# A hybrid decoder layer on one core: two projections in half-size products over all sixteen feature tiles, with seventeen early weight tiles

## The chip, the cores and the metric

The kernel runs on one core of a Trainium2 chip. The metric is the device time of one execution in microseconds (us); less is better. Engines: TensorE (PE) for matrix products, VectorE (DVE) and ScalarE (ACT) for elementwise work, GpSimd (POOL) and SyncE (SP) for little more than the issue of transfers. A "cast" below is ACT's copy of an fp32 tile to the rounded format that PE multiplies.

## The reference

One decoder layer for x of 512 tokens by 2048 features, in float32:

```python
h = rmsnorm(x, g)
p = h @ w_in                      # (512, 2048) @ (2048, D_IN), split by IN_SPLITS
# attention group: q, keys and values for three branches, branch gates, a gate path z_a of 1024 columns
# HGRN2 group: q, forget gate f, values i (1024 columns), a gate path z_h
o = concat(nsa(...) * silu(z_a), hgrn2(...) * silu(z_h))   # each head normalised first
y = rmsnorm(x + o @ w_out, g_final)
```

What matters here are two of the column groups of w_in, each of 1024 columns: HGRN2's values (from column C_IH on) and the attention's gates (from C_ZA on). Each is a product of h (512 x 2048) with a 2048 x 1024 piece of w_in.

## The kernel before

**Precision.** Every fp32 operand is split in two rounded parts, a high part (the cast, L304, on ACT) and a low part (the rest, L305, on DVE); the function is parts(), and a product takes three matmuls: high by high, high by low, low by high. The transposed, normalised input lies in SBUF as hh and hl, sixteen feature tiles of 128 x 512 each.

**The order of the program.** Small projections of the keys and values come first (second_proj and proj_tm, up to L586), then the two large projections of this case in seven products each, then blocks() (L611 to L625), make_kd, make_q and the compression of keys and values (L632 to L641), then attention, HGRN2 and the output. Each engine works off its own list of instructions in order; the lists are made when the program is built, from the order of the code and from when buffers come free.

**Seven products.** seven() (L406) splits a 512 x 1024 projection in a 2 x 2 block form: the tokens in two halves of 256, the columns in two halves of 512, and the feature tiles in pairs, of which one member is the first and the other the second half of the inner dimension. By Strassen's rule in Winograd's form seven half-size products do for eight; their left operands are sums of blocks of the input (sums_of, L365 to L377, made once, while the projection of V runs), their right operands sums of weight blocks. PAIRS says how many pairs of feature tiles go this way, 6 of 8 before; the last four feature tiles go through rest(), as plain products into the same banks.

A projection is a list of steps, each with a part that prepares and a part that multiplies. Two pairs make a step. first(jj) loads three weight blocks of 128 x 1024 (L419), makes two differences (L410) and three pairs of parts; it feeds three products. second(jj) and third(jj) load one block, add one (L411), and make two pairs of parts for two products each. A step of rest() loads one block (L163) and makes one pair of parts for 24 plain matmuls (L466 to L468). The half-size products stand at L456 to L458. in_turn() runs the steps and prepares AHEAD7 = 2 steps ahead of the step that multiplies, over both projections in one list. After a group of steps the sums of the products are taken out of PSUM: after_first, after_second, after_third, after_all, by DVE additions (L411 again, on 128 x 512 tiles called e), and then scaled (L535, v_done) or put through a tanh (L541 and L542, z_done). third_sums() keeps one corner of the input aside in DRAM and writes a sum over it; block_21_back() (L401) brings it back during the second projection.

**Buffers.** Weight tiles are 128 x 1024 in float32, 4 KB a partition. b4() takes them by turns from two pools, w with WBUF = 10 tiles and, in this first part of the kernel, more_w with NU = 10. The space of more_w and of the sums goes to other tiles after the two projections.

**Behind the projections.** blocks() brings the keys for compression back from DRAM with eight transfers that ACT issues (L611 to L614) and adds position vectors to them on DVE (L625, sixteen additions). make_kd(0, 0) and make_q(0) project keys and queries with weight tiles of eight feature tiles by 128 columns (proj_fm, L559 to L561, two tiles a projection, 24 matmuls a tile); split_dma (L686 to L691) then spreads the result over partitions by transfers that SP issues. compress() (L632 to L641) loads its own weights through SP too.

Of the kernel before, what the change touches and what calls it, by code (L numbers as in the profile page):

```python
# [30 lines left out]
WBUF = 10  # L31
# [2 lines left out]
PJ = 4  # L34
AHEAD = 2
FILL = (44, 42, 40, 24)
NU = 10
NE = 8
PAIRS = 6
AHEAD7 = 2  # L40
KWB = 4
EVA = "AD"
# [6 lines left out]
def hymba_layer(ctx: ExitStack, tc: tile.TileContext, x, norm_in, w_in, pe_k, w1_k, w2_k,  # L49
# [12 lines left out]
    cnt = [0, 0, 0]  # L62

    def nm(s):
        cnt[0] += 1
        return f"{s}_{cnt[0]}"


    space, first_part = {}, ExitStack()
# [11 lines left out]
    def dram(shape=(P, 512)):  # L81
        n = nm("d")
        return scr.tile(list(shape), FP32, name=n, tag=n, bufs=1)
# [6 lines left out]

    def b4(dt):
        cnt[2] += 1
        if "more_w" in space and cnt[2] % 2:
            return space["more_w"].tile([P, WCOLS], dt, name=nm("w"), tag="w", bufs=NU)
        return space["w"].tile([P, WCOLS], dt, name=nm("w"), tag="w", bufs=WBUF)

# [64 lines left out]
    def load_raw(src, k0, kt, c0, c):  # L161
        raw = b4(FP32)[:, 0:kt * c].rearrange("p (k c) -> p k c", k=kt)
        nc.sync.dma_start(out=raw, in_=src[k0 * P:(k0 + kt) * P, c0:c0 + c].rearrange("(k p) c -> p k c", p=P))  # L163
        return raw
# [4 lines left out]
    for k0, kt in FIRST:  # L169
        cs = slice(k0 * P, (k0 + kt) * P)  # L170
        first_w.append(load_raw(w_in2, k0, kt, C_KC, 256))
        if kt == 2:
            w = b4(FP32).rearrange("p (t c) -> p t c", t=4)
            for i in range(2):
                nc.sync.dma_start(out=w[:, 2 * i:2 * i + 2],
                                  in_=x2[i * 256:(i + 1) * 256, cs].rearrange("(t p) c -> p t c", p=P))
            xt.append([w[:, t] for t in range(NT)])
        else:
            w = [b4(FP32).rearrange("p (t c) -> p t c", t=2) for _ in range(2)]
            xt.append([w[t // 2][:, t % 2] for t in range(NT)])  # L180
            for t in range(NT):
                nc.sync.dma_start(out=xt[-1][t], in_=x2[t * P:(t + 1) * P, cs])
# [125 lines left out]
    def load_w(src, k0, kt, c0, c, to=None):  # L308
        return parts(load_raw(src, k0, kt, c0, c), to)
# [43 lines left out]

    a21 = [[dram((P, 2, 256)) for _ in range(PAIRS // 2)] for _ in range(2)]
    sums, s3 = {}, {}
# [28 lines left out]
    def all_sums():  # L384
        for j in range(PAIRS):
            sums_of(j)
            yield 1.0

    def third_sums():

        for q in range(PAIRS // 2):
            for part in range(2):
# [5 lines left out]
    def block_21_back():  # L398
        for q in range(PAIRS // 2):
            for part in range(2):  # L400
                nc.gpsimd.dma_start(out=corner(q, part).bitcast(FP32), in_=a21[part][q])  # L401
# [4 lines left out]
    def seven(c0, done, then=lambda: None):  # L406
# [36 lines left out]
        def give(*names):  # L443
            for name in names:
                free_banks.append(banks[name])

        def products(jj, ops, names):
            for (left, bank, fresh), (hi, lo) in zip(names, ops):
                if jj == 0 and fresh:
                    take(bank)  # L450
                for tt in range(2):
                    ts = slice(tt * P, (tt + 1) * P)
                    o = acc[bank][tt]
                    for j in range(2):
                        ah, al = [a[:, ts] for a in sums[2 * jj + j][left]]
                        nc.tensor.matmul(o, ah, hi[:, j], start=fresh and jj + j == 0, stop=False, skip_group_check=True)  # L456
                        nc.tensor.matmul(o, al, hi[:, j], start=False, stop=False, skip_group_check=True)  # L457
                        nc.tensor.matmul(o, ah, lo[:, j], start=False, stop=jj + 1 == PAIRS // 2 and j == 1,  # L458
                                         skip_group_check=True)

        def plain(k0, w, outs):
            hi, lo = w
            for t in range(NT):
                for k in range(2):
                    ah, al = [hT[part][k0 + k][:, t * P:(t + 1) * P] for part in range(2)]
                    nc.tensor.matmul(outs[t], ah, hi[:, k], start=False, stop=False, skip_group_check=True)  # L466
                    nc.tensor.matmul(outs[t], al, hi[:, k], start=False, stop=False, skip_group_check=True)
                    nc.tensor.matmul(outs[t], ah, lo[:, k], start=False, stop=k0 + k == NK - 1, skip_group_check=True)  # L468
# [20 lines left out]
        def after_third():  # L489
            for tt in range(2):  # L490
                add(room["u2"][tt], acc["5"][tt], room["u2"][tt])

        def after_all():
            for tt in range(2):
                y = room["u2"][tt]
                add(y, acc["3"][tt], y)
                done(1, tt, y, y)
            for tt in range(2):
                y = room["u3"][tt]
                add(y, acc["5"][tt], y)  # L500
                done(1, 2 + tt, y, y)
            give("5", "3")

        def group(prepare, names, after):
            steps = [(lambda jj=jj: prepare(jj), lambda ops, jj=jj: products(jj, ops, names)) for jj in range(PAIRS // 2)]
            return steps[:-1] + [(steps[-1][0], lambda ops: (steps[-1][1](ops), after()))]

        def rest(right, names, after):
            steps = []
            for k0 in range(2 * PAIRS, NK, 2):  # L510
                def mul(w, k0=k0):
                    plain(k0, w, [acc[n][tt] for n in names for tt in range(2)])
                    if k0 + 2 == NK:
                        after()
                steps.append((lambda k0=k0: load_w(w_in2, k0, 2, c0 + 512 * right, 512), mul))
            return steps

        return (group(first, (("A11", "1", True), ("S2", "6", True), ("S3", "7", True)), after_first) +
                group(second, (("A22", "4", True), ("A12", "1", False)), lambda: None) + rest(0, "14", after_second) +
                group(third, (("S1", "5", True), ("S4", "3", True)), after_third) + rest(1, "35", after_all))  # L520
# [632 lines left out]
    with tc.manual_schedule(engines={mybir.EngineType.PE, mybir.EngineType.Activation, mybir.EngineType.DVE}):  # L1153
# [5 lines left out]
         70), (all_sums(), 7))  # L1159
    third_sums()  # L1160
    in_turn(seven(C_IH, v_done) + seven(C_ZA, z_done(0), block_21_back))
    first_part.close()
    del space["more_w"]
# [139 lines left out]
```

## Time and profile before

| | us |
|---|---|
| median of three runs | 1102.68 |
| lowest and highest run | 1102.62, 1103.29 |
| the profiled execution | 1100.78 |
| its span | 1099.1 |
| PE busy in it | 1073.5 (98%) |
| DVE busy | 658.8 (60%) |
| ACT busy | 419.6 (38%) |
| POOL busy | 95.5 (9%) |

The span runs from the first to the last instruction of the profiled execution, the time of an execution has a little around it. The mean granted clock of PE in it was 0.994 of full speed. Shares of busy time are averages over stages that differ; what a stage waits for is read from the timeline of that stage. Matmuls overlap: one of 512 columns lasts 0.39 us in the timeline, and the next starts 0.23 us behind it.

### The profile page before, as it was taken

What the parts mean: (1) busy time and instruction counts of PE and PEld (TensorE: products, weight loads), DVE (VectorE), ACT (ScalarE), POOL (GpSimd) and SP (SyncE); (2) the same over time, 40 slices, a digit from 0 to 9 for tenths busy, and PEclk for the clock granted to TensorE, in tenths of its full rate; (3) what the DMA queues carried; (4) which work ended last, traced back from release to release, by engine and by line L of the source; (5) the groups of instructions that cost most, each with busy time, mean ns of one, the idle gap of its engine ahead of it and who ended that gap; (6) DMA issues with size and microseconds to landing.
All of it is one profiled execution on the core that took longest, in us unless ns stands there. A gap on an engine that the chain in (4) does not pass through costs nothing.

```text
span 1099.1 us, 15254 instructions
## 1 busy us (share of the span) xinstructions
PE 1073.5 (98%) x5610; PEld 883.3 (80%) x5610; DVE 658.8 (60%) x1549; ACT 419.6 (38%) x835; POOL 95.5 (9%) x170
## 2 busy tenths in 40 slices
PE   7999999999989999999999999999999999999996
PEld 6799888888868777777877887888888888888886
DVE  4767656764344676576765565666666788424332
ACT  6534443442123665555553222222222443324211
POOL 1000000101521020110200000000000000202010
PEclk9999999999999999999999999999999999999999
DMA  9435346444685222222212323221222723335223
GB/s 317 146 119 161 118 134 209 155 163 130 195 267 139 71 61 59 62 73 58 58 40 78 95 68 105 78 77 58 77 61 63 248 90 106 113 109 172 96 86 124
DMA packets 100010, 127.45 MB, mean 116 GB/s; under 512 B 6672, under 2 KB 62368, under 8 KB 99936
## 3 DMA queue, kind: packets, MB, share of 16 engines
q1 hardware_dynamic: 94368, 113.90, 33.8%
q0 software_dynamic: 2624, 8.39, 2.1%
q10 hardware_dynamic: 2944, 4.19, 1.1%
q8 instruction: 44, 0.72, 0.3%
q14 instruction: 30, 0.25, 0.1%
HBM read 106.01 MB, written 12.06 MB: 107 GB/s over the span
## 4 chain that ended last, share of the span: by engine, by line
PE 90%; DVE 5%; DMA 2%; issue 2%; ACT 1%; SPq 0%; ACTq 0%; POOL 0%; DVEq 0%; POOLq 0%
PE pj L559 8%; PE pj L560 8%; PE pj L561 8%; PE pj L584 7%; PE pj L586 7%; PE pj L585 7%; PE ot L826 4%; PE pj L807 3%; PE lp L975 2%; PE pj L458 2%; PE pj L457 2%; PE pj L456 2%; PE lp L793 2%; PE lp L641 2%; PE lp L794 1%
## 5 line engine op out<-in xcount | busy, mean ns | idle before, releaser
L305 DVE TENSOR_TENSOR w<-w,w 128x1024 fp32r<-128x1024 f32 (+3 forms) x169 | 204.4, 1215 | 188.9 <-ACT w L304 88.3
L304 ACT CAST w<-w 128x1024 fp32r<-128x1024 f32 (+3 forms) x169 | 173.0, 1036 | 276.3 <-DMA w<-in_w_in_dram 148.4
L559 PE MATMUL pj<-hh,w 128*128 128x512 f32 x448 | 183.5, 410 | 2.8 <-ACT w L304 2.2
L560 PE MATMUL pj<-hl,w 128*128 128x512 f32 x448 | 178.6, 399 | 0.0
L561 PE MATMUL pj<-hh,w 128*128 128x512 f32 x448 | 176.7, 394 | 0.5 <-DVE w L305 0.5
L584 PE MATMUL pj<-w,hh 128*128 128x512 f32 (+2 forms) x352 | 127.1, 361 | 0.0
L585 PE MATMUL pj<-w,hl 128*128 128x512 f32 (+2 forms) x352 | 125.8, 358 | 0.0
L586 PE MATMUL pj<-w,hh 128*128 128x512 f32 (+2 forms) x352 | 125.6, 357 | 0.0
L559 PEld LDWEIGHTS pj<-hh,w 128*128 128x128 f32 x448 | 84.3, 188 | 21.1 <-issue 2.9
L561 PEld LDWEIGHTS pj<-hh,w 128*128 128x128 f32 x448 | 84.2, 188 | 19.0 <-issue 1.2
L560 PEld LDWEIGHTS pj<-hl,w 128*128 128x128 f32 x448 | 84.4, 188 | 15.9 <-issue 1.3
L767 ACT ACTIVATE s<-s,mn 128x128 f32<-128x128 f32 (+3 forms) x128 | 71.6, 560 | 28.1 <-DVE mn L762 18.6
L762 DVE CUSTOM_DVE_ANT_0 s<-s,lp 128x128 f32<-128x128 f32 (+3 forms) x128 | 60.3, 482 | 35.9 <-PE lp L794 32.8
L586 PEld LDWEIGHTS pj<-w,hh 128*128 128x128 f32 x352 | 66.5, 189 | 8.5
L584 PEld LDWEIGHTS pj<-w,hh 128*128 128x128 f32 x352 | 66.5, 189 | 8.1
L585 PEld LDWEIGHTS pj<-w,hl 128*128 128x128 f32 x352 | 66.5, 189 | 8.0
L807 PE MATMUL pj<-ident,s 128*128 128x128 f32 x320 | 53.8, 274 | 0.4 <-ACT s L767 0.3
L816 ACT COPY pt<-pj 128x256 f32<-128x256 f32 (+2 forms) x56 | 25.6, 457 | 57.4 <-PE pj L807 57.2
L826 PE MATMUL ot<-pt,s 128*64 128x512 f32 (+3 forms) x256 | 47.3, 440 | 0.0
L807 PEld LDWEIGHTS pj<-ident,s 128*128 128x128 f32 x320 | 39.6, 140 | 9.5 <-ACT s L767 3.0
L826 PEld LDWEIGHTS ot<-pt,s 128*64 128x64 f32 x256 | 22.8, 136 | 21.2 <-issue 11.3
L584 PE MATMUL pj<-w,s 128*128 128x512 f32 x96 | 37.7, 392 | 0.0
(346 smaller groups left out, 1912.0 us busy)
## 6 DMA issues: line engine op xcount, KB each, us to landing
w<-in_w_in_dram SPq DMA_DIRECT2D x121, 512.0 KB, 3.5
w<-in_w_out_dram SPq DMA_DIRECT2D x32, 512.0 KB, 3.6
s<-s SPq DMA_DIRECT2D x48, 128.0 KB, 2.3
w<-in_x_dram SPq DMA_DIRECT2D x16, 256.0 KB, 6.4
d<-e POOLq DMA_DIRECT2D x12, 256.0 KB, 3.1
l<-in_x_dram SPq DMA_DIRECT2D x12, 256.0 KB, 5.1
out_dram<-l SPq DMA_DIRECT2D x12, 256.0 KB, 3.1
w<-in_w_in_dram SPq DMA_DIRECT2D x5, 456.0 KB, 3.2
```

The costliest lines, as they stand in the source:

```text
L304: nc.scalar.copy(hi, raw)
L305: nc.vector.tensor_tensor(lo, raw, hi.bitcast(FP32), ALU.subtract)
L559: nc.tensor.matmul(acc[j], wh, hh, start=kk == 0, stop=False)
L560: nc.tensor.matmul(acc[j], wh, hl, start=False, stop=False)
L561: nc.tensor.matmul(acc[j], wl, hh, start=False, stop=kk == NK - 1)
L584: nc.tensor.matmul(o, ah, hi[:, k, :], start=kk == 0, stop=False)
L585: nc.tensor.matmul(o, al, hi[:, k, :], start=False, stop=False)
L586: nc.tensor.matmul(o, ah, lo[:, k, :], start=False, stop=kk == NK - 1)
L762: nc.vector.tensor_tensor_reduce(out=y, in0=e["bias"][:, 384 - i * P:512], in1=lp, scale=1.0, scalar=3e38, op0=ALU.add, op1=ALU.min, accum ...
L767: nc.scalar.activation(y, y, AF.Exp, bias=mn, scale=-1.0, accum_out=e["ls"][:, 2 * i + b:2 * i + b + 1])
L807: nc.tensor.transpose(tps[:, j * P:(j + 1) * P], y[:, j * P:(j + 1) * P], ident)
L826: nc.tensor.matmul(e["ot"][b * 64:(b + 1) * 64, j * P:512], v_tok[j][:, b * 256 + g * DH:b * 256 + (g + 1) * DH], e["pt"][:, b, j * 512:38 ...
```

## The change

All sixteen feature tiles go through the half-size products: PAIRS is 8, each group has four steps in place of three, and rest() is empty. The sums of two more pairs of the input are made and kept, which takes 12 KB a partition; more_w has seven tiles in place of ten, and b4() deals the tiles out in the ratio of seven to ten. Without steps in rest(), after_second comes behind the second group itself, and after_third and after_all come together behind the third. All lines behind L517 move down by 4.

```diff
--- before.py
+++ after.py
@@ -34,9 +34,9 @@
 PJ = 4
 AHEAD = 2
 FILL = (44, 42, 40, 24)
-NU = 10
+NU = 7
 NE = 8
-PAIRS = 6
+PAIRS = 8
 AHEAD7 = 2
 KWB = 4
 EVA = "AD"
@@ -90,7 +90,7 @@
 
     def b4(dt):
         cnt[2] += 1
-        if "more_w" in space and cnt[2] % 2:
+        if "more_w" in space and cnt[2] * NU % (NU + WBUF) < NU:
             return space["more_w"].tile([P, WCOLS], dt, name=nm("w"), tag="w", bufs=NU)
         return space["w"].tile([P, WCOLS], dt, name=nm("w"), tag="w", bufs=WBUF)
 
@@ -515,6 +515,10 @@
                 steps.append((lambda k0=k0: load_w(w_in2, k0, 2, c0 + 512 * right, 512), mul))
             return steps
 
+        if not rest(0, "14", None):
+            return (group(first, (("A11", "1", True), ("S2", "6", True), ("S3", "7", True)), after_first) +
+                    group(second, (("A22", "4", True), ("A12", "1", False)), after_second) +
+                    group(third, (("S1", "5", True), ("S4", "3", True)), lambda: (after_third(), after_all())))
         return (group(first, (("A11", "1", True), ("S2", "6", True), ("S3", "7", True)), after_first) +
                 group(second, (("A22", "4", True), ("A12", "1", False)), lambda: None) + rest(0, "14", after_second) +
                 group(third, (("S1", "5", True), ("S4", "3", True)), after_third) + rest(1, "35", after_all))
```

A projection has 336 matmuls in place of 348. The lists of the engines change most at two places, and SP's behind them. In the rows below w is a weight tile, e an eviction tile of 128 x 512, pj, lp, tp and ot PSUM banks, s a tile of the second part, d scratch in DRAM; the number behind a name tells tiles of one kind apart. L535, L541, L542, L611 and L625 of before are L539, L545, L546, L615 and L629 of the change.

**DVE, from the end of the first projection to the start of the second.** Before:

```order
L305 TENSOR_TENSOR w_1725<-w_1719,w_1724 128x1024
L305 TENSOR_TENSOR w_1729<-w_1722,w_1728 128x1024
L411 TENSOR_TENSOR e_1422<-pj_1625,e_1422 128x512
L411 TENSOR_TENSOR e_1423<-pj_1626,e_1423 128x512
L305 TENSOR_TENSOR w_1733<-w_1717,w_1732 128x1024
L410 TENSOR_TENSOR w_1762<-w_1762,w_1760 128x1024
L410 TENSOR_TENSOR w_1767<-w_1762,w_1764 128x1024
L305 TENSOR_TENSOR w_1770<-w_1764,w_1769 128x1024
L305 TENSOR_TENSOR w_1774<-w_1767,w_1773 128x1024
L305 TENSOR_TENSOR w_1778<-w_1762,w_1777 128x1024
L411 TENSOR_TENSOR e_1422<-lp_1639,e_1422 128x512
L411 TENSOR_TENSOR e_1423<-lp_1640,e_1423 128x512
```

The sums over e_1422 to e_1425 are after_third and after_all of the first projection; w_1725 to w_1733 are low parts of the first step of the second projection, w_1762 to w_1778 its second step. Both steps stand ahead of the last sums. With the change:

```order
L411 TENSOR_TENSOR e_1514<-pj_1693,e_1514 128x512
L411 TENSOR_TENSOR e_1516<-pj_1693,e_1516 128x512
L411 TENSOR_TENSOR e_1515<-pj_1694,e_1515 128x512
L411 TENSOR_TENSOR e_1514<-lp_1707,e_1514 128x512
L410 TENSOR_TENSOR w_1758<-w_1758,w_1756 128x1024
L411 TENSOR_TENSOR e_1515<-lp_1708,e_1515 128x512
L410 TENSOR_TENSOR w_1763<-w_1758,w_1760 128x1024
L305 TENSOR_TENSOR w_1766<-w_1760,w_1765 128x1024
L411 TENSOR_TENSOR e_1517<-pj_1694,e_1517 128x512
L305 TENSOR_TENSOR w_1770<-w_1763,w_1769 128x1024
L305 TENSOR_TENSOR w_1774<-w_1758,w_1773 128x1024
```

Here e_1514 to e_1517 are the sums and w_1758 to w_1774 the first step of the second projection. The sum over lp_1708 waits for the last product of the first projection, and the subtraction that makes w_1763 and the low parts w_1766, w_1770 and w_1774 stand behind it.

**ACT, at the same place.** Before, the casts of the first two steps and then the scalings of the last sums:

```order
L304 CAST w_1724<-w_1719 128x1024
L304 CAST w_1728<-w_1722 128x1024
L304 CAST w_1732<-w_1717 128x1024
L304 CAST w_1769<-w_1764 128x1024
L304 CAST w_1773<-w_1767 128x1024
L304 CAST w_1777<-w_1762 128x1024
L535 ACTIVATE e_1422<-e_1422,rs 128x512
L535 ACTIVATE e_1423<-e_1423,rs 128x512
L536 DMA d_160<-e_1422 128x512
L536 DMA d_161<-e_1423 128x512
```

With the change:

```order
L304 CAST w_1728<-w_1721 128x1024
L304 CAST w_1724<-w_1368 128x1024
L539 ACTIVATE e_1516<-e_1516,rs 128x512
L540 DMA d_164<-e_1516 128x512
L539 ACTIVATE e_1514<-e_1514,rs 128x512
L540 DMA d_162<-e_1514 128x512
L304 CAST w_1765<-w_1760 128x1024
L539 ACTIVATE e_1515<-e_1515,rs 128x512
L304 CAST w_1769<-w_1763 128x1024
L304 CAST w_1773<-w_1758 128x1024
L540 DMA d_163<-e_1515 128x512
```

The scaling of e_1514, whose sum is the fourth row on DVE above, stands ahead of the cast w_1765, which the first product of the second projection takes.

**ACT, from the second projection to make_kd.** Before, four weight tiles of make_kd and make_q, then the last tanhs and the transfers of blocks():

```order
L304 CAST w_2445<-w_2443 128x1024
L304 CAST w_2475<-w_2473 128x1024
L304 CAST w_2524<-w_2522 128x1024
L304 CAST w_2554<-w_2552 128x1024
L541 ACTIVATE e_2332<-e_1976,rs 128x512
L541 ACTIVATE e_2337<-e_1977,rs 128x512
L541 ACTIVATE e_2342<-e_1978,rs 128x512
L611 DMA s_2364<-d_500 64x512
```

With the change:

```order
L545 ACTIVATE e_2385<-e_2076,rs 128x512
L616 DMA s_2417<-d_502 64x511
L545 ACTIVATE e_2390<-e_2077,rs 128x512
L545 ACTIVATE e_2395<-e_2078,rs 128x512
L545 ACTIVATE e_2400<-e_2079,rs 128x512
L617 DMA s_2418<-d_502 64x512
L618 DMA s_2418<-d_502 64x511
L615 DMA s_2423<-d_503 64x512
L616 DMA s_2423<-d_503 64x511
L617 DMA s_2424<-d_503 64x512
L618 DMA s_2424<-d_503 64x511
L304 CAST w_2528<-w_2526 128x1024
```

The tiles w_2445 and w_2475 of before are the two of make_kd(0, 0), w_2524 and w_2554 those of make_q(0). The other seven transfers and the fourth tanh follow behind. With the change w_2498 and w_2528 are the two of make_kd(0, 0); w_2498 and one transfer stand just ahead of these rows, and w_2528 stands behind all eight transfers.

**DVE, at the same place.** Before:

```order
L305 TENSOR_TENSOR w_2446<-w_2443,w_2445 128x1024
L305 TENSOR_TENSOR w_2476<-w_2473,w_2475 128x1024
L411 TENSOR_TENSOR e_1976<-pj_2193,e_1976 128x512
L411 TENSOR_TENSOR e_1977<-pj_2194,e_1977 128x512
L305 TENSOR_TENSOR w_2525<-w_2522,w_2524 128x1024
L305 TENSOR_TENSOR w_2555<-w_2552,w_2554 128x1024
L411 TENSOR_TENSOR e_1976<-pj_2207,e_1976 128x512
L411 TENSOR_TENSOR e_1977<-pj_2208,e_1977 128x512
L542 SCALAR_TENSOR_TENSOR e_1976<-e_2332,e_1976 128x512
```

With the change:

```order
L305 TENSOR_TENSOR w_2499<-w_2496,w_2498 128x1024
L411 TENSOR_TENSOR e_2077<-pj_2286,e_2077 128x512
L546 SCALAR_TENSOR_TENSOR e_2076<-e_2385,e_2076 128x512
L546 SCALAR_TENSOR_TENSOR e_2077<-e_2390,e_2077 128x512
L546 SCALAR_TENSOR_TENSOR e_2078<-e_2395,e_2078 128x512
L546 SCALAR_TENSOR_TENSOR e_2079<-e_2400,e_2079 128x512
L629 TENSOR_TENSOR s_2429<-s_2417,col 128x4x31
L629 TENSOR_TENSOR s_2429<-s_2418,col 128x4x31
...
L629 TENSOR_TENSOR s_2432<-s_2423,col 128x4x31
L305 TENSOR_TENSOR w_2529<-w_2526,w_2528 128x1024
L629 TENSOR_TENSOR s_2429<-s_2424,col 128x4x31
```

The low parts w_2446, w_2476, w_2525 and w_2555 stood ahead of the last sums. With the change only w_2499 does; w_2529, the low part of make_kd's second tile, stands behind twelve rows of L629.

**SP, from make_kd to the compression.** L163 loads weights, L632 compression's, L691 spreads kd (64 rows a transfer). Before:

```order
L163 DMA w_2552<-in_w_in_dram 128x8x128
L163 DMA w_2595<-in_w_in_dram 128x8x128
L632 DMA w_2613<-in_cmp_w_k_dram 128x4x256
L632 DMA w_2628<-in_cmp_w_k_dram 128x4x256
L632 DMA w_2650<-in_cmp_w_k_dram 128x4x256
L691 DMA s_2503<-s_2508 64x512 x2
L691 DMA s_2504<-s_2509 64x512 x2
L691 DMA s_2505<-s_2508 64x512 x2
```

With the change, where L636 and L695 are these lines:

```order
L163 DMA w_2605<-in_w_in_dram 128x8x128
L163 DMA w_2648<-in_w_in_dram 128x8x128
L695 DMA s_2556<-s_2561 64x512 x2
L695 DMA s_2557<-s_2562 64x512 x2
L695 DMA s_2558<-s_2561 64x512 x2
L695 DMA s_2559<-s_2562 64x512 x2
L636 DMA w_2666<-in_cmp_w_k_dram 128x4x256
L636 DMA w_2681<-in_cmp_w_k_dram 128x4x256
```

Three of the compression's weight tiles stood ahead of the transfers that spread kd; with the change all of them stand behind.

## Rows read from the trace of the kernel before

**Rows 1.** The page: busy time by engine, granted clock in 40 slices, chain that ended last.

```profile
PE 1073.5 (98%) x5610; PEld 883.3 (80%) x5610; DVE 658.8 (60%) x1549; ACT 419.6 (38%) x835; POOL 95.5 (9%) x170
...
PEclk9999999999999999999999999999999999999999
...
PE 90%; DVE 5%; DMA 2%; issue 2%; ACT 1%; SPq 0%; ACTq 0%; POOL 0%; DVEq 0%; POOLq 0%
```

**Rows 2.** Windows: us; busy PE, PEld, DVE, ACT, POOL (count); clock, DMA share, GB/s.

```profile
70.00:112.60 42.60, 42.60 (x326) 42.60 (x325) 24.55 (x34) 16.55 (x28) 0.00 (x0) 1.00 0.45 144
...
112.80:270.10 157.30, 157.30 (x695) 130.26 (x694) 100.22 (x99) 61.23 (x69) 7.01 (x11) 1.00 0.46 148
...
300.00:318.00 18.00, 18.00 (x99) 15.43 (x98) 6.06 (x10) 3.87 (x7) 6.43 (x19) 1.00 0.87 259
...
326.00:330.00 4.00, 2.62 (x12) 2.65 (x13) 4.00 (x12) 1.04 (x1) 0.00 (x0) 0.50 0.33 100
330.00:334.00 4.00, 4.00 (x27) 4.00 (x26) 1.24 (x2) 1.04 (x1) 0.00 (x0) 0.68 0.00 0
```

**Rows 3.** Timeline of PE: start, us, work; where the two projections begin and end.

```profile
112.57 0.39 PE L456 MATMUL pj<-w,hh 128*128 128x512 f32 x1
...
270.14 0.39 PE L468 MATMUL pj<-w,hh 128*128 128x512 f32 x1
270.36 0.39 PE L559 MATMUL pj<-hh,w 128*128 128x512 f32 x1
```

**Rows 4.** DVE by line and shape, 112.6 to 270.2: busy us, mean ns | idle before.

```profile
L305 DVE TENSOR_TENSOR w<-w,w 128x1024 fp32r<-128x1024 f32 x49 | 59.1, 1222 | 38.0 <-ACT w L304 25.4 <-PE pj L468 5.2 <-PE pj L458 4.0
L411 DVE TENSOR_TENSOR w<-w,w 128x1024 f32<-128x1024 f32 x12 | 14.6, 1220 | 2.0 <-DMA w<-in_w_in_dram 2.0
L411 DVE TENSOR_TENSOR e<-pj,e 128x512 f32<-128x512 f32 x15 | 10.3, 690 | 6.3 <-PE pj L458 3.9 <-PE pj L468 2.0
```

**Rows 5.** ACT by line and shape in the same stretch.

```profile
L304 ACT CAST w<-w 128x1024 fp32r<-128x1024 f32 x48 | 48.8, 1050 | 80.3 <-DVE w L411 37.1 <-DMA w<-in_w_in_dram 27.5 <-DVE w L410 8.2
L535 ACT ACTIVATE e<-e,rs 128x512 f32<-128x512 f32 x6 | 4.3, 724 | 6.1 <-DVE e L411 6.1
```

**Rows 6.** Timeline of PE near the end of the first projection, one product.

```profile
188.54 0.39 PE L468 MATMUL lp<-w,hh 128*128 128x512 f32 x1
```

**Rows 7.** Timeline of DVE: the sum that waits for it.

```profile
188.96 0.69 DVE L411 TENSOR_TENSOR e<-lp,e 128x512 f32<-128x512 f32 x1 [0.67 <-PE lp L468]
```

**Rows 8.** Timeline of ACT (ACTq: its issues) behind the second projection.

```profile
270.56 0.50 ACTq L611 DMA_DIRECT2D s<-d  x1
...
275.74 0.62 ACTq L614 DMA_DIRECT2D s<-d  x1
276.40 1.05 ACT L304 CAST w<-w 128x1024 fp32r<-128x1024 f32 x1 [4.39 <-issue]
```

**Rows 9.** Timeline of DVE at the same place.

```profile
277.28 3.85 DVE L625 TENSOR_TENSOR s<-s,col 128x124 f32<-128x124 f32 x11 [2.47 <-DMA s<-d]
281.05 1.22 DVE L305 TENSOR_TENSOR w<-w,w 128x1024 fp32r<-128x1024 f32 x1
```

**Rows 10.** Timeline of PE, 321 to 328.5 us.

```profile
321.36 0.39 PE L561 MATMUL pj<-hh,w 128*128 128x512 f32 x1
323.91 0.50 PE L559 MATMUL pj<-hh,w 128*128 128x512 f32 x1 [2.15 <-ACT w L304]
...
325.17 0.50 PE L561 MATMUL pj<-hh,w 128*128 128x512 f32 x1 [0.52 <-DVE w L305]
...
327.38 1.41 PE L641 MATMUL lp<-s,w 128*128 128x128 f32 x5 [1.46 <-issue]
```

**Rows 11.** The chain that ended last, 300 to 330 us: start, us, what.

```profile
314.40 8.31 DMA w<-in_w_in_dram
```

**Rows 12.** Timeline of SP's issues, 270 to 325 us.

```profile
284.81 5.02 SPq L691 DMA_DIRECT2D s<-s x8
```

## Prediction

> **What bounds the kernel now.** I read the page first. TensorE (PE) is busy for 98% of the span, and the chain that ended last runs through it for 90%, with 5% on VectorE (DVE) [rows 1]. So time is won by fewer matmuls, and lost where PE has to stand still. The windows show how this holds in the part that changes: from 112.8 to 270.1 us, the two projections in seven products, PE is busy for all of the 157.30 us at a granted clock of 1.00, DVE for 100.22 and ScalarE (ACT) for 61.23 [rows 2]. The timeline gives the price of a matmul there: the first starts at 112.57, the first of make_kd behind them at 270.36, with 2 x (252 + 96) = 696 between them and no gap [rows 3]: (270.36 - 112.57) / 696 = 0.2267 us each. The operands are prepared by ACT and DVE only a little ahead, so that gapless stretch rests on an order of work that the change disturbs. The one place near here where PE does stand still is at 321 to 328 us [rows 10]; it supplies the prices for what follows a wait.
>
> **The products: -5.4.** With eight pairs a projection has 7 operands x 4 steps x 12 matmuls = 336, where it had 7 x 3 x 12 = 252 and four groups of 24 for the rest, 348. Both projections: 24 fewer, 24 x 0.2267 = 5.4 us, all on the path. The Trainium skill, TensorE: Matmul & The Clock Gate, section Back-to-back issue gap, gives about 131 ns for a 512-column matmul in a stream of weight loads and matmuls; this trace does not agree, at 226.7, and by that figure the term would be an estimated 3.1 (24 x 0.131).
>
> **What is added beside PE: 0 by amount.** In both projections together there are 6 more casts on ACT (1.05 each, 6.3 us [rows 5]), 6 more low parts and 8 more adds or subtractions on DVE (14 x 1.22 = 17.1 us [rows 4]), and 2 more loads. DVE would be busy for 117.3 us of 151.9, 77%: not a bound by itself. The sums of two more pairs come ahead, while the matmuls of V run: seven DVE operations a pair, none larger than the 1.22 of a 128x1024 addition, so at most 17 us, and DVE had 42.60 - 24.55 = 18 us free in the last stretch before the products alone [rows 2]. If that cover were gone, the first products would wait for the last sums; I allow 0 to 1 us for this and take 0. The order decides the rest, at two seams.
>
> **Seam 1, between the two projections: +3.3.** Before, the rest products (24 matmuls a group) stood between the last operand of one projection and the first of the next; the cast and the parts of the next first group stood ahead of the last sums on DVE, and PE ran on. Now the last sums stand in front of these parts. On DVE, the sum e_1515 waits for the very last product; behind it come the subtraction w_1763, and the low part w_1766 that the next projection's fifth matmul takes. A sum starts 0.42 us after the start of the product that it waits for (188.54 to 188.96 [rows 6, 7]) and takes 0.69; so counted from the start of the last product the low part is there at 0.42 + 0.69 + 1.23 + 1.22 = 3.56, or 4.1 if the subtraction w_1758 ahead of the sum ends later than the product. PE would want it at 5 x 0.2267 = 1.13. That is a wait of 2.4 to 3.0. (The cast of the same tile stands on ACT behind the scaling of e_1514, whose product comes six earlier: -6 x 0.2267 + 0.42 + 0.69 + 0.72 [rows 5] + 0.50 for a transfer's issue [rows 8] + 1.05 = 2.0, wanted at 0.23; 1.8 of the wait are there already.) The next low part, w_1770, stands behind one more sum (0.69): I put 0.3 for it. Taken 3.3, ends 2.4 and 4.0. Inside the projections the parts have 1.4 us and more to spare; only in the second, one cast of the third group stands on ACT behind a tanh whose input comes from a late product. I put **+0.7** there (0 to 2).
>
> **Seam 2, from the second projection to make_kd: +6.1.** Here make_kd(0, 0) wants two weight tiles of eight feature tiles each, 24 matmuls a tile. Before, both of them and the two of make_q were cast and split ahead of the last sums. Now only the first is (w_2498, w_2499). The second's cast, w_2528, stands on ACT behind the eight DMA issues of blocks(); its low part, w_2529, on DVE behind twelve additions of blocks() that wait for these DMAs. The trace shows what that costs, counted from the last product at 270.14 [rows 3]: the issues start at 270.56 and the cast behind them at 276.40, +6.26, so it ends at +7.31 [rows 8]; the additions start at 277.28 when the DMAs have landed, the low part follows at 281.05, and it ends at +12.1 [rows 9]. There it was the third tile, which nobody wanted yet. Now PE has 24 matmuls of cover, until 0.22 + 24 x 0.2267 = +5.7; it waits for the cast until +7.3, runs two matmuls with it, and from +7.8 waits for the low part until +12.1: 1.6 + 4.4 = 6.0, with 0.1 for the step behind it. Ends: 5.5, if the DMAs land half a microsecond sooner, and 7.7, if DVE gets to the additions later.
>
> **What follows a wait of that length: +2.5.** After 321.36 PE waited for a cast (2.15), a low part (0.52) and once more (1.46), 4.1 in all [rows 10]. The granted clock fell to 0.50 in the windows at 326 to 330 and stood at 0.68 on average in the next four us [rows 2]; these are its 1.2 GHz level and a mix with 2.4 GHz. The loss: 2.62 us of busy PE at half speed, 1.3, and 4.00 x 0.32 = 1.3, in sum 2.6 (3.4 if all eight us counted). Seam 2 is the same pattern, only longer: two waits with two matmuls between them. I take 2.5 there, ends 0 and 3.4; at seam 1, half as long, 0, and 2 for the upper end. The Trainium skill, same page, section What's actually happening, says that the throttled state is the default and that activity releases it. The trace agrees: 0.50 after this idle time, 1.00 before it. By that rule the change has a cost that the matmul count doesn't show.
>
> **Behind make_kd: +2.3.** On SP the compress weights, once issued ahead of the eight DMAs that spread kd (5.02 us for eight [rows 12]), now stand behind them: +0.8, ends 0 and 3. The wait at 321 us came from a weight load that took 8.31 us from its issue at 314.40 [rows 11]. The tile that takes this load now is the second half of make_kd(0, 1), which has about 26 matmuls in front of it instead of 48; (48 - 26) x 0.2267 = 5.0 less cover, but the load is issued sooner by a part of this. I put +1.5. Ends: -6.7, if the later PE gives the load its time and the 4.1 of waiting and 2.6 of clock go, and +5.0.
>
> **The sum**: -5.4 + 3.3 + 0.7 + 6.1 + 2.5 + 0.8 + 1.5 = +9.5. The profiled execution took 1100.78 (span 1099.1), 1.9 below the median of the three runs, 1102.68; I add to the median: 1112.2, so **1112 us**.
>
> **The rivals.**
> (a) *The waits, without their consequences.* The clock stays full through seam 2 and the work behind it absorbs its new order: -5.4 + 3.3 + 0.7 + 6.1 = +4.7, 1107.4. For it: two matmuls run between the waits, and PE keeps a clock of 1.00 everywhere else. Against it: the fall at 325 to 333 us after waits shorter than these.
> (b) *Faster, since the old wait goes.* The load that landed at 322.7 was the one late piece before; a PE that comes 4.7 later finds it there, and 4.1 + 2.6 are won back: 4.7 - 6.7 = -2.0, 1100.7. It decides if the load's issue does not move along with PE. Against it: the load stands on SP behind the split of q, which itself waits for PE's result, so issue and PE move together.
> (c) *The orders at the seams don't bind*, as the parts arrive in time after all: only the products count, 1102.7 - 5.4 = 1097.3. It would need the last sum before the last product, so I give it little. That fewer products are not there at all the counts above exclude: 672 against 696 in PE's list.
> (d) *Worse.* Both seams throttle, at the upper ends: -5.4 + 4.0 + 2 + 7.7 + 3.4 + 2 + 3 + 1.5 = +18.2, 1121.
>
> **How the numbers follow.** The forecast, both seams and the clock, 1108.5 to 1117: 0.55. (a), between 1105 and 1108.5: 0.20. Between these and no change, by small ends of all terms or half of (b): 0.08. (b) and (c), faster by over 0.2%: 0.05 and 0.03. (d), from 1117: 0.09. About 0.2%, 2.2 us, is what a measurement of this kernel can tell from no change, so within 0.2% is 1100.5 to 1104.9. Slower: 0.55 + 0.20 + 0.09 = 0.84, same 0.08, faster 0.08. The range leaves out (b), (c) and the far half of (d): 1101 to 1119.
>
> **What the next profile would show.** PE: 672 instead of 696 product matmuls at 0.227. On the timeline, PE idle for about 3 us at the start of the second projection (near 188.7), released by the cast at L304 and then by DVE L305; and some 6 us in two pieces about 6 us behind the last product, released by the same two, with a clock near 0.5 in the four us after. The first compress matmuls and the second half of make_kd(0, 1) wait as long as before or longer. I would be wrong if PE runs through both seams gapless (then the orders on ACT and DVE don't bind), if the wait at seam 2 is there but the end of the kernel doesn't move by it (then something later was waiting anyway), or if the waits inside the projections are more than 2 us.

## The result, and the profile after

The changed kernel is slower: a median of 1118.48 us over four executions, 1114.6 to 1118.63, beside 1102.65 (1102.23 to 1103.29). The ratio is 1.0133, with a 95% interval from 1.0121 to 1.0146, that is +13.3 to +16.1 us. The profiled execution is the fastest of the four, 1114.6, with a span of 1112.9 and a mean granted clock of 0.990; the other three lie at 1118.4 to 1118.6, at a clock of 0.988, and what they have more is in no trace. What follows accounts for the 13.8 us between the two spans. Since the trace lies 3.9 us below the median, a median held against 1118.48 shows up to 4 us more gain than the traces do; where that matters below, both are given.

The page of the changed kernel, its busy times (to be held against [rows 1]):

```profile
PE 1071.1 (96%) x5586; PEld 877.7 (79%) x5586; DVE 680.0 (61%) x1578; ACT 427.2 (38%) x846; POOL 99.4 (9%) x174
```

There are the 24 matmuls less, and DVE has 21 us more; PE's share fell from 98% to 96% of a longer span, so PE stands still more. Where, the windows tell (stretch, us, busy time of PE, PEld, DVE, ACT, POOL with counts, granted clock, DMA share, GB/s; as in [rows 2]):

```profile
111.60:267.60 156.00, 153.33 (x672) 125.45 (x672) 111.33 (x109) 64.00 (x72) 7.91 (x12) 1.00 0.49 157
...
270.00:274.00 4.00, 4.00 (x19) 3.16 (x17) 3.59 (x9) 1.57 (x4) 4.00 (x13) 1.00 0.75 206
274.00:278.00 4.00, 0.95 (x3) 0.30 (x2) 2.26 (x7) 1.99 (x2) 4.00 (x6) 0.95 0.98 321
278.00:282.00 4.00, 1.73 (x4) 1.44 (x5) 4.00 (x10) 0.59 (x1) 4.00 (x7) 0.50 1.04 355
282.00:286.00 4.00, 4.00 (x14) 3.11 (x14) 0.70 (x1) 0.46 (x1) 4.00 (x9) 0.70 0.03 9
...
324.00:328.00 4.00, 0.39 (x2) 0.00 (x0) 0.36 (x1) 0.00 (x0) 3.32 (x10) 1.00 1.01 272
328.00:332.00 4.00, 0.00 (x0) 0.00 (x0) 2.26 (x9) 0.00 (x0) 0.54 (x1) 0.60 1.11 296
332.00:336.00 4.00, 0.00 (x0) 0.00 (x0) 1.94 (x8) 1.00 (x1) 0.00 (x0) 0.50 0.99 336
336.00:340.00 4.00, 3.91 (x20) 3.72 (x21) 2.45 (x2) 1.09 (x2) 0.00 (x0) 0.62 0.40 114
```

From their first matmul to the first of make_kd the two projections take 156.29 us where they took 157.79, only 1.5 less for 24 matmuls less. Then there are two holes: one at 274 to 282, behind the second projection, and a large one at 324 to 336, where PE does nothing for twelve us while the DMA engines are full. In both, the clock goes to 0.50. On PE's timeline (start, us, work, in brackets the idle time and what ended it):

```profile
187.53 0.39 PE L458 MATMUL lp<-w,s 128*128 128x512 f32 x1
189.60 0.50 PE L456 MATMUL tp<-w,hh 128*128 128x512 f32 x1 [1.68 <-ACT w L304]
...
191.35 0.50 PE L458 MATMUL tp<-w,hh 128*128 128x512 f32 x1 [0.56 <-DVE w L305]
...
267.63 0.39 PE L458 MATMUL pj<-w,s 128*128 128x512 f32 x1
...
268.93 0.50 PE L565 MATMUL pj<-hh,w 128*128 128x512 f32 x1 [0.46 <-DVE w L305]
...
275.00 0.50 PE L563 MATMUL pj<-hh,w 128*128 128x512 f32 x1 [0.78 <-ACT w L304]
275.33 0.40 PE L564 MATMUL pj<-hl,w 128*128 128x512 f32 x1
280.27 0.80 PE L565 MATMUL pj<-hh,w 128*128 128x512 f32 x1 [4.54 <-DVE w L305]
...
324.00 0.39 PE L565 MATMUL pj<-hh,w 128*128 128x512 f32 x1
336.09 0.80 PE L563 MATMUL pj<-hh,w 128*128 128x512 f32 x1 [11.70 <-ACT w L304]
```

In brackets, the first two waits are seam 1, the next three seam 2, as the prediction placed them; the last answers to [rows 10], with 11.7 us in place of 2.15 + 0.52 + 1.46. At seam 2 ACT's timeline shows the cast directly behind the last of eight transfers, and DVE's shows the low part behind the additions (L629):

```profile
272.60 1.25 ACTq L618 DMA_DIRECT2D s<-d  x1
273.90 1.05 ACT L304 CAST w<-w 128x1024 fp32r<-128x1024 f32 x1 [2.43 <-issue]
```

```profile
273.14 2.48 DVE L629 TENSOR_TENSOR s<-s,col 128x124 f32<-128x124 f32 x7 [0.41 <-DMA s<-d]
277.36 1.59 DVE L629 TENSOR_TENSOR s<-s,col 128x124 f32<-128x124 f32 x4 [1.74 <-DMA s<-d]
278.87 1.34 DVE L305 TENSOR_TENSOR w<-w,w 128x1024 fp32r<-128x1024 f32 x1
```

Counted from the last product at 267.63, the cast ends at +7.3 and the low part at +12.6; [rows 8] and [rows 9] gave +7.3 and +12.1. At the late load, SP's timeline and ACT's cast of that tile:

```profile
319.88 2.52 SPq L695 DMA_DIRECT2D s<-s  x4
322.44 0.59 SPq L636 DMA_DIRECT2D w<-in_cmp_w_v_dram  x1
323.13 0.64 SPq L163 DMA_DIRECT2D w<-in_w_in_dram  x1
```

```profile
335.00 1.04 ACT L304 CAST w<-w 128x1024 fp32r<-128x1024 f32 x1 [14.42 <-DMA w<-in_w_in_dram]
```

The load is issued at 323.13, behind the four transfers that spread the second pair of queries and a tile of the compression; PE has its last matmul ahead of it at 324.00. It lands 11.8 us later. Before, the load that was late was issued at 314.40, 7 us ahead of PE's last matmul at 321.36, and took 8.31 [rows 11]. So the load is issued 6.1 us later as PE's work goes and takes 3.5 longer; together that is the 9.6 by which the wait for its cast grew, from 2.15 to 11.70. In both kernels POOL begins shortly ahead of the load to issue twelve transfers of its own (the row of the first, with the change and before):

```profile
321.27 0.56 POOL L615 DMA_DIRECT2D s<-d  x1
```

```profile
311.84 0.56 POOL L611 DMA_DIRECT2D s<-d  x1
```

The load follows 1.9 us behind that start with the change and 2.6 before, so the burst alone hardly tells the two apart. What differs is the tile of the compression, as large as the load and issued 0.7 us ahead of it with the change alone. How much of the 3.5 us comes from which was not tried.

### The profile page after: what moved, and what is told of

It is laid out like the page before. It is cut to its first block, busy times and chain, and to the rows that moved or that the text cites. A ratio compares the mean times of both kernels' runs of the same rounds, so it can differ in the third digit from the quotient of the medians.

```text
span 1112.9 us, 15271 instructions
## 1 busy us (share of the span) xinstructions
PE 1071.1 (96%) x5586; PEld 877.7 (79%) x5586; DVE 680.0 (61%) x1578; ACT 427.2 (38%) x846; POOL 99.4 (9%) x174
## 5 line engine op out<-in xcount | busy, mean ns | idle before, releaser
L305 DVE TENSOR_TENSOR w<-w,w 128x1024 fp32r<-128x1024 f32 (+3 forms) x175 | 210.2, 1212 | 160.6 <-ACT w L304 70.3
L304 ACT CAST w<-w 128x1024 fp32r<-128x1024 f32 (+3 forms) x175 | 179.1, 1037 | 256.8 <-DMA w<-in_w_in_dram 138.4
L563 PEld LDWEIGHTS pj<-hh,w 128*128 128x128 f32 x448 | 84.9, 189 | 32.7 <-ACT w L304 14.1
```

The costliest lines, as they stand in the source:

```text
L304: nc.scalar.copy(hi, raw)
L305: nc.vector.tensor_tensor(lo, raw, hi.bitcast(FP32), ALU.subtract)
L563: nc.tensor.matmul(acc[j], wh, hh, start=kk == 0, stop=False)
```

## The experiments

Twelve kernels ran, each five rounds beside the kernel before on the same chip; all compute the whole layer. The kernel before had medians of 1102.62, 1102.61 and 1101.77 in the three groups of runs (e1 to e4, e5 to e8, e9 to e12), each group on another chip; the changed kernel itself ran in none of them, and "less than the change" below is against its median of 1118.48.

**e1: fewer tiles alone.** The kernel before, with

```diff
-NU = 10
+NU = 7
-        if "more_w" in space and cnt[2] % 2:
+        if "more_w" in space and cnt[2] * NU % (NU + WBUF) < NU:
```

> The kernel before with 17 early weight tiles dealt out in the new ratio, and nothing else. Theory A (the waits come from the missing rest steps, which leave only one weight tile of make_kd ahead of the transfers of blocks): three of make_kd's and make_q's tiles are still cast and split ahead, so within 2 us of 1102.7. Theory B (fewer tiles delay the preparation by themselves): most of the loss, 1108 or more, with waits of PE behind L304 inside or between the projections.

Measured: 1109.0 (1106.69 to 1110.8), ratio 1.0057 (1.0041 to 1.0073). Neither theory has it. PE runs through both seams without a wait, so no tile is late there, as theory A says. But the time is 6 us longer, and PE's timeline shows where:

```profile
318.12 0.39 PE L561 MATMUL pj<-hh,w 128*128 128x512 f32 x1
330.36 0.79 PE L559 MATMUL pj<-hh,w 128*128 128x512 f32 x1 [11.84 <-ACT w L304]
```

It is the late load of the changed kernel, in a kernel without its products. SP's list shows the difference to before. Before:

```
L632 DMA w_2834<-in_cmp_w_v_dram 128x4x256
L163 DMA w_2844<-in_w_in_dram 128x8x128
L691 DMA s_2713<-s_2716 64x512
L691 DMA s_2713<-s_2717 64x512
L691 DMA s_2714<-s_2716 64x512
L691 DMA s_2714<-s_2717 64x512
L163 DMA w_2930<-in_w_in_dram 128x8x128
```

and with 17 tiles:

```
L691 DMA s_2713<-s_2716 64x512
L691 DMA s_2713<-s_2717 64x512
L691 DMA s_2714<-s_2716 64x512
L691 DMA s_2714<-s_2717 64x512
L632 DMA w_2834<-in_cmp_w_v_dram 128x4x256
L163 DMA w_2844<-in_w_in_dram 128x8x128
```

The tile w_2844, and one of the compression, went from ahead of the queries' four transfers to behind them. The wait for it is the loss. In the traces, between the first matmul of make_kd and the first of attention's values, this kernel takes 101.37 us where the one before takes 92.39, 9.0 more, and PE's idle time there is 8.9 more. (The medians differ by 6.4: the trace of the kernel before lies 1.9 below its median, that of e1 0.9 above.)

**e2 and e3: eight pairs in one projection only.** The edit gives seven() its own number of pairs; the sums of all eight pairs and the 17 tiles stay.

```diff
-    def seven(c0, done, then=lambda: None):
+    def seven(c0, done, then=lambda: None, pairs=PAIRS, end=lambda: None):
...
-    in_turn(seven(C_IH, v_done) + seven(C_ZA, z_done(0), block_21_back))
+    in_turn(seven(C_IH, v_done) + seven(C_ZA, z_done(0), block_21_back, pairs=6))
```

That is e2; in e3 the first has pairs=6, and the last corner's sums are written behind it, by end.

> The sums of eight pairs and 17 tiles as in the change, but only the first projection in eight pairs; the second keeps six pairs and its rest steps. So seam 1 is as in the change and seam 2 as before. Theory A: products -2.7, start of the section -1.0 as in the change's trace, seam 1 +2.6, some 0.6 for the third tile behind seam 2: -0.5, 1102 (1100 to 1105). Theory B (tiles): 1108 or more. Theory C (the long wait for the late weight load has nothing to do with seam 2): it is there too, 1109 or more.

> The mirror of it: six pairs and rest steps in the first projection, eight in the second, so seam 2 as in the change and seam 1 as before. Theory A: -2.7 -1.0 for products and start, +1.2 inside the second projection, +6.3 and +2.3 of clock at seam 2, and +9 at the late load behind it: +15, 1117 (1113 to 1119). If the late load is not a consequence of seam 2: about 1108.

Measured: e2 1116.72 (1115.47 to 1118.35), ratio 1.0132 (1.0116 to 1.0149); e3 1114.82 (1113.16 to 1115.15), ratio 1.0111 (1.0095 to 1.0127). Seam 1 is where it should be: e2 has the waits of 1.68 and 0.56 between the projections, e3 none there. Seam 2 is not what was asked for in either. e3 has waits of 2.48 and 1.21 there, 3.7 in sum, where the change has 0.46, 0.78 and 4.54. And e2, whose second projection keeps its rest steps, still takes 30.36 us from make_kd's first matmul to the compression, 5.9 more than the kernel before and e1 (24.49 and 24.48), with waits of 0.95, 2.01 and 0.53 that neither of those has; so eight pairs in the first projection, with the sums kept for them, cost time behind the second as well, and why was not tried. The longest of these in e2:

```profile
295.36 0.50 PE L564 MATMUL pj<-hh,w 128*128 128x512 f32 x1 [2.01 <-ACT w L304]
```

Both have the late load, whole, as e2's largest wait (us in total, times, longest) and e3's show:

```profile
PE pj L564 <- ACT w L304: 14.6, 2, 12.6
```

```profile
PE pj L564 <- ACT w L304: 12.7, 2, 11.7
```

So theory A, that this wait follows from seam 2, falls, and theory C of e2's expectation stands. e3 agreed in size (1117 forecast), for reasons that were not its own.

**e4: blocks() later.**

```diff
-    kblk = blocks(kf, 32, nc.scalar)
...
-    run((chain(make_kd(0, 0), make_q(0)), 22))
+    kd00 = make_kd(0, 0)
+    for _ in range(3):
+        next(kd00)
+    kblk = blocks(kf, 32, nc.scalar)
+    run((chain(kd00, make_q(0)), 22))
```

> The change with blocks() of the compressed keys issued after three pieces of make_kd(0, 0), so that the cast and the low part of make_kd's second tile stand ahead of the eight transfers and the twelve additions. All theories: the waits of 0.9 and 4.7 us at seam 2 and the 2.3 of clock behind them go. If the late load's wait of 11.7 us is a thing of its own (a tile fewer ahead on SP, and a burst of transfers from POOL): 1118.5 - 8 = 1110.5. If it follows from the wait at seam 2: 1103 or less.

Measured: 1113.67 (1112.22 to 1114.68), ratio 1.0103 (1.0087 to 1.0119): 4.8 less than the change, not 8. The two long waits at seam 2 are down to one of 0.34 us, but PE now stands still for 2.86 us ahead of the compression's first matmul, and the late load is unmoved at 11.8. That it doesn't follow from seam 2 is shown a second time. The gain itself is less sure than the 4.8: the trace of e4 takes 108.17 us from make_kd's first matmul to attention's values where that of the change takes 109.23, and the two spans are the same (1113.0 and 1112.9).

**e5 and e6: the queries' four transfers on ACT.** The same edit to the change (e5) and to the kernel before (e6):

```diff
-    def split_dma(acc_ps, scale, dsts):
+    def split_dma(acc_ps, scale, dsts, eng=nc.sync):
...
-            nc.sync.dma_start(out=dst[half_ * 64:half_ * 64 + 64, :].bitcast(FP32),
+            eng.dma_start(out=dst[half_ * 64:half_ * 64 + 64, :].bitcast(FP32),
...
-        split_dma(acc[0], -DH ** -0.5, [(qe, 0, 0, 0), (qe, 1, 1, 0), (qo, 0, 0, 1), (qo, 1, 1, 1)])
+        split_dma(acc[0], -DH ** -0.5, [(qe, 0, 0, 0), (qe, 1, 1, 0), (qo, 0, 0, 1), (qo, 1, 1, 1)],
+                  nc.scalar if p in (1,) else nc.sync)
```

> The change, but the four transfers that spread the second pair of queries (make_q(1)) are issued by ACT in place of SP, so that the late weight load doesn't stand behind them. Theory D (the load's buffer is free at about 315.5 us, when PE has used the compression's last key tile, but the load waits on SP until 323.1 behind the four transfers, and then shares the DMA engines with POOL's burst that begins at 321.3): the load starts at about 316 and lands near 320, before PE wants it at 324; 11.7 us and some 2 us of clock go: 1105 (1103 to 1108). Rival E (it is the burst, not the place on SP): PE still waits 5 us or more there, 1111 or more.

> The same edit on the kernel before. Theory D: the waits of 4.1 us at 321 to 328 and their 2.6 us of clock go: 1096 (1095 to 1099). Rival E: no change, 1102 to 1103.

Measured: e5 1108.16 (1107.57 to 1109.17), ratio 1.0051 (1.0039 to 1.0063), 10.3 less than the change (6.4 between the spans); e6 1095.75 (1095.13 to 1097.68), ratio 0.994 (0.9928 to 0.9952), **faster than both kernels**. The load goes earlier in both, as theory D had it; e6 lies inside its bounds, e5 just above its own. In e6 only 0.86 us is left of the waits at 321 to 328. In e5 SP issues the load at once when the compression's keys are done (PE's last sixteen matmuls of it run from 315.77 to 317.55):

```profile
317.59 3.13 SPq L163 DMA_DIRECT2D w<-in_w_in_dram  x2
```

and PE's wait there falls from 11.7 to 3.3 us, for another reason, which the chain of waits names in e5 (start, us, what): the low part stands on DVE behind an addition of blocks(), which waits for a transfer of POOL.

```profile
324.88 3.49 DMA s<-d
...
328.46 0.06 DVE s L629
...
328.74 1.23 DVE w L305
...
330.01 0.50 PE pj L565
```

That is seam 2's pattern once more, with the compressed values in place of the keys, and why e5 came out above its bounds. The load left two things behind at once: the four transfers, and POOL's burst, which in e5 begins only at 323.29. So rival E in its strong form is out, but what the burst alone costs isn't shown.

**e7: one tile more, two eviction tiles fewer.**

```diff
-NU = 7
-NE = 8
+NU = 8
+NE = 6
```

> The change with eight tiles in more_w in place of seven, paid for with two eviction tiles (six in place of eight). The three casts of the second projection's first step then stand ahead of the scalings at seam 1. Theory A (order at the seam): the 2.2 us of waits there go, the rest stays as in the change: 1116 (1114 to 1117). If seam 1's waits hang on the weight loads and not on the order of the casts: 1118.5, with the waits still there.

Measured: 1117.39 (1116.56 to 1117.61), ratio 1.0132 (1.0119 to 1.0146), hardly less than the change (2.6 more between the spans) and just above theory A's bounds. The three casts now stand ahead, and the waits of 1.68 and 0.56 at seam 1 are gone; PE reaches make_kd 1.8 us earlier relative to the section's start (154.5 against 156.3). But there it waits 2.1 for the first low part, where it waited 0.46. What was won at seam 1 is waited away behind it: from make_kd's first matmul to the compression it takes 35.92 us in place of 33.07.

**e8: the three edits together** (e7, e4 and e5).

> The change with all three edits: eight tiles in more_w and six eviction tiles, blocks() behind three pieces of make_kd(0, 0), and the queries' transfers on ACT. If the three causes add up: 1118.5 - 2.2 - 4.8 (as measured for blocks alone) - 13.5 = 1098, faster than the kernel before by 0.4%; that would be all of the products' 5.4 us. If a wait behind one takes the place of another: 1101 to 1106.

Measured: 1108.73 (1106.88 to 1109.68), ratio 1.0052 (1.0039 to 1.0064), no better than e5 alone and above both forecasts: a wait took the place of another. PE's waits for low parts in all of make_kd and make_q, in total, times and longest:

```profile
PE pj L565 <- DVE w L305: 12.1, 5, 4.5
```

The second tile of make_kd is now ahead of blocks(), and the third tile, make_q's first, stands behind it and costs the 4.5 in its place.

**e9 and e10: the additions on POOL.** In blocks(), for the keys (e9), or for keys and values and with e5's edit (e10):

```diff
-    def blocks(acc, pcol, eng):
+    def blocks(acc, pcol, eng, adder=nc.vector):
...
-                nc.vector.tensor_tensor(b4_[:, :, g, 0:31], sv, pe, ALU.add)
+                adder.tensor_tensor(b4_[:, :, g, 0:31], sv, pe, ALU.add)
...
-    kblk = blocks(kf, 32, nc.scalar)
+    kblk = blocks(kf, 32, nc.scalar, nc.gpsimd)
```

> The change, with the sixteen additions of the compressed keys' blocks() made by POOL in place of DVE, and nothing else; DVE's low part of make_kd's second tile then stands behind no addition. If that queue on DVE is what makes seam 2 long: the wait of 4.5 us for the low part falls to about 0.6 (cast done, low part 1.2 behind it, two matmuls of cover), the 2.3 us of clock behind it go, the late load stays: 1112 (1111 to 1114). If POOL's slower additions delay the compression as much: 1116 or more.

Measured: e9 1114.5 (1113.26 to 1115.02), ratio 1.0115 (1.0101 to 1.0129), 4.0 less than the change by the medians, and no less by the spans (1113.3 and 1112.9). The low part follows the cast directly, so the queue on DVE was what it waited for. Its stage, from make_kd's first matmul to the compression, takes 30.13 us in place of 33.07. But PE's wait falls to 2.26 only, not 0.6, because the low parts themselves got slower. DVE by line and shape in e9, 275 to 284 us (busy us, mean ns), and PE's wait:

```profile
L305 DVE TENSOR_TENSOR w<-w,w 128x1024 fp32r<-128x1024 f32 x2 | 4.4, 2214 | 2.2 <-ACT w L304 2.2
```

```profile
278.62 0.50 PE L565 MATMUL pj<-hh,w 128*128 128x512 f32 x1 [2.26 <-DVE w L305]
```

They take 2214 ns on the mean while POOL adds beside them, and 1222 elsewhere [rows 4]; the first of the two, which PE waits for, took 2961, and these 1.74 us more are about what stands between 2.26 and the forecast.

> The change with both blocks() added on POOL and the second queries' transfers on ACT. From the 1108.2 of the run with the transfers alone: -4 to -6 for seam 2 as above, and -3.3 for the wait that remained behind the late load, if that too is a low part behind the additions of the compressed values: 1099 (1097 to 1103). If waits only move on: 1106 or more.

Measured: e10 1107.4 (1106.92 to 1107.89), ratio 1.0053 (1.0039 to 1.0067), a miss: hardly less than e5. The waits move on: the compression of the values now waits for POOL, and the matmul behind it on PE with it.

```profile
329.72 0.58 PE L645 MATMUL lp<-s,w 128*128 128x128 f32 x1 [5.32 <-POOL s L629]
```

**e11 and e12: the same with one tile more, and on the kernel before.**

> The same with eight tiles in more_w and six eviction tiles, which took the waits at seam 1 away (2.2 us): 1097 (1095 to 1101). If there is one tile too few behind the second projection in any case: as the run without it.

> The kernel before with the same two edits. It has nothing left to gain at seam 2, where PE didn't wait; so as with the transfers on ACT alone, 1095.8 (1095 to 1097). If the additions on DVE held up something else: faster than 1095. The difference to the run of the change with the same edits is what the eight pairs are worth once the two queues are mended: -5.4 if the products alone count, above zero if the seams still cost more than that.

Measured: e11 1109.4 (1106.89 to 1110.49), ratio 1.0066 (1.0053 to 1.0079), no better than e10: the tile helps at seam 1 alone, as in e7. e12 1098.46 (1097.4 to 1099.85), ratio 0.9969 (0.9958 to 0.9981): above its bounds and slower than e6, since the values' compression waits 3.3 us for POOL. With the same edits in both, the eight pairs with their 17 tiles cost 1108.16 - 1095.75 = 12.4 us (e5 and e6) or 1107.4 - 1098.46 = 8.9 (e10 and e12); pairs and tiles are not told apart by this. No version of them came near 1095.75.

## Why the prediction was right, and where it was mis-sized

It forecast +9.5 us in a range of 1101 to 1119, with 0.84 for slower; measured were +13.8 between the spans and +15.8 between the medians, at 1118.48, near the range's end. That time lies in the stretch from 1117 on that the prediction gave to its rival (d), with 0.09: the direction was right, and the range held the size by the room left for (d). Step by step, in us, from the starts of the same matmuls in both traces (first product, first of make_kd, first of the keys' compression, first of attention's values, end):

| step | forecast | in the traces |
|---|---|---|
| products | -5.4 | -5.4 (24 matmuls less) |
| start of the section | 0 | -1.0 (first product 112.57 to 111.57; over all the runs, with and without eight pairs, it lies anywhere from 111.4 to 113.4, so this is no gain of the change) |
| seam 1 | +3.3 | +2.6 (1.84 + 0.72) |
| inside the projections | +0.7 | +1.4 (what is left of 156.29 - 157.79) |
| seam 2 | +6.1 | +6.3 (0.61 + 0.94 + 4.71) |
| clock behind it | +2.5 | +2.3 (33.07 from make_kd's first to the compression, less 24.49 before, less 6.26) |
| behind make_kd | +2.3 | +8.3 (76.16 against 67.90 from the compression's first to attention) |
| the rest | 0 | -0.5 |

**The products and the seams** went as forecast: the two engines' lists that were read for them held, and the times of [rows 6 to 9] carried over within 0.5 us. e2 shows seam 1's waits by themselves, e3 their absence, and e9 that the queue on DVE is what makes seam 2 long: its low part follows the cast at once. **The clock** fell to 0.50 behind seam 2 and not at seam 1, as put. (The 3.4 named for all eight us counted is 3.3: 4.00 x 0.50 + 4.00 x 0.32.)

**The step that was mis-sized is the last**, "I put +1.5" for the wait at 321 us, beside the +0.8 for the compression's weights. The two together measured +8.3, and nearly all of it is the load's: its wait is 11.70 where the three waits of [rows 10] are 4.13, and 1.1 stand at 310 us for an earlier tile. PE doesn't wait ahead of the compression's first matmul, so of the +0.8 nothing shows. That is above the upper end of 5.0 for this wait; the mechanism, less cover in front of a load that stands behind the queries' transfers, was the one named. Two things were missed. The cover lost was taken to be partly made good by an earlier issue; the load was in fact issued only 0.9 us ahead of PE's last matmul, where it had been 7. And its time to land was taken as fixed: it took 11.8 us in place of 8.31.

**What the prediction had no name for** is the part of the change that brings this wait. It gave the new order of SP's list and its price, but not what in the change makes it; the first expectations of e2 to e4 weighed seam 2 as the cause. e1 has no eight pairs and has the wait all the same, e4 mends seam 2 and keeps it. It comes with the 17 tiles: two loads fall behind the four transfers on SP's list. Why three early tiles fewer move the list so was not tried. e5 shows that the place on SP's list decides most of it: 11.7 us fell to 3.3 without any change of buffers.

**The rivals.** (a), without consequences, is out: both came. (b), that the old wait goes, is out, for the issue moved by more than PE's need, 8.7 us later (314.40 to 323.13) against 2.6 (321.36 to 324.00). (c) is out. (d) had both seams throttle; its 1121 is close to the time measured, but by luck: the late load made it, and not the clock at seam 1, which stayed at 1.00.

The parts don't add up. By the medians the tiles alone cost 6.4 us, eight pairs in the first projection with them 14.1, in the second 12.2, in both 15.8; a saving of 2.2 at seam 1 (e7) gave 1.1, and three edits gave no more than one (e8 and e5). Behind the second projection PE is fed tile by tile through one order on ACT, DVE and SP, and who comes earlier waits there. Between e5 and e6 the traces put 9.6 us into the stretch from make_kd's first matmul to the compression (34.05 and 24.48) and 7.7 into the one from there to attention's values (68.33 and 60.64), beside 1.5 won in the projections; the spans differ by 10.5, the medians by 12.4. What stays open: the 4 us by which three executions of the change are longer than the profiled one, why e2 loses time behind the second projection, and what in the 3.5 us by which the late load lands slower is the burst's.

## What to carry to other kernels

Price fewer matmuls together with the work that they covered: the removed plain steps were cheap to prepare and let the next stage's tiles be ready ahead, and without them the next stage's first tiles stood behind eight transfers on ACT and twelve waiting additions on DVE. Look for the transfer that is already late in the kernel before, and don't carry its time over as a constant; here four transfers on another engine's queue were worth more (6.9 us, e6) than all of the saved products (5.4). And when buffers pay for a change, run the smaller pool by itself first.

## What the runs showed of the hardware that was not expected

DVE's 128x1024 subtraction, 1222 ns in the projections [rows 4], took 2214 ns on the mean of two while POOL made its additions (e9; 2120 in e10). The Trainium skill, GPSIMD Engine Reference, section Specifications, says that POOL's access to SBUF is shared with VectorE, with contention when a DVE instruction has two SBUF inputs; the subtraction has two, and the trace agrees, with a factor of 1.8. So work that is moved from DVE to POOL can slow the DVE work that it was to make room for.

A 512 KB load issued inside POOL's burst of twelve transfers took 8.31 us before and 11.8 in the change, there behind another load of its size and with the DMA engines at a share of 0.99 to 1.11 from 324 to 336.
